# First FFN of a hybrid decoder layer: temporaries in other room, masks in one tile, activation differences on VectorE, output evictions two products later

## The chip, the cores and the metric

The kernel runs on one core of one Trainium2 chip. The metric is the device time of one execution in microseconds (us). The engines are TensorE (PE, with its weight loads as PEld), VectorE (DVE), ScalarE (ACT), GpSimd (POOL) and SyncE (SP, which here only issues DMAs).

## What is computed

One layer on 1024 tokens of width 1024, with 16 learned meta tokens ahead of them, everything in float32:

```python
h = h + 0.5 * swiglu(rms_norm(h, ffn1_norm[l]), ffn1_w_in[l], ffn1_w_out[l])
u = rms_norm(h, mix_norm[l]) @ w_in[l]
hq, hf, hi, hg, sq, sk, sv = jnp.split(u, ...)
o_hg = hgrn2(hq, hf, hi, hg, lb_all[l], hgrn_out_norm[l], valid)
o_sb = stick_breaking(sq, sk, sv, sb_q_norm[l], sb_k_norm[l], valid)
h = h + jnp.concatenate([o_hg, o_sb], axis=-1) @ w_out[l]
h = h + 0.5 * swiglu(rms_norm(h, ffn2_norm[l]), ffn2_w_in[l], ffn2_w_out[l])

def swiglu(h, w_in, w_out):          # D_FF = 2816
    g, u = jnp.split(h @ w_in, 2, axis=-1)
    return (jax.nn.silu(g) * u) @ w_out
```

## The kernel before

**Exactness.** Each float32 operand of a product is split into a rounded high part and a low remainder. ACT casts the high part and DVE subtracts it to get the low one: L360 and L362 for the weights of the first FFN (`wh`, `wl`), L310 and L311 for its activations (`halve`), L612 and L613 in the output pass (`w`, `t`). A product takes three passes, high by high, low by high and high by low. With four blocks of 128 in the contraction, one product of the FFN is 12 matmuls of 128x512.

**Products by halves.** The two FFNs are computed with seven products in the place of eight, on operands divided in halves (a Strassen-Winograd scheme). The activation's halves are B11, B21, B22 and the combinations T1, T2, T3, T4. Weights are combined by POOL (L384, `s`) and activations by DVE. In `fast_in`, a *quad* is the 2x2 blocks of one gate or up column group, and a *pair* is a gate quad and an up quad. The 22 column groups of the first FFN are 11 pairs, named 0 to 10 here. The results of a quad are put together in PSUM banks qa, qb and qc (L430). `u2` (L462) reads the bank qb after the product T2, ahead of the product T3, which adds to the same bank. ACT applies silu, and DVE multiplies gate and up into `sg`.

The products of a pair, `act` B11 to B22, go to DRAM and are read again by the output pass. `combined()` also makes the four combinations T1 to T4 of these. Its subtractions are L533 (T1, T2, T4) and L540 (T3), its DMAs L529. The tile `t` that holds T1, T2 and T4 has two buffers (`t_bufs`, 2), so T4 takes T1's buffer. In the kernel before, both the subtractions and the DMAs are on POOL.

**The opening.** `open_tokens` loads the token rows, scales them by their norm, turns them on PE, and makes T1 to T4 and B11 to B22. Pairs 0 to 3 are the *openers*. Their eight quads take part in the opening: the products B11 and B21 come first, while the second half of the tokens is still prepared, then T2 for each quad, and after `open_ev()` the rest, in turns of a gate and an up quad (`in_turns`). The temporaries `b11, b21, b22, t2, t3` lie in a pool `temps`. At the end of `open_tokens` come the halves of T1, T4 and B22. `open_ev()` then closes `temps` and opens three pools in its room: `ev1` (tiles of the evictions), `turn` and `early` (raw weight blocks of openers' up quads). The causal masks of the later attention are cut by POOL with affine selections on one tile `sd`, one level of seven after the other (L129, L133), each begun by a memset on DVE and ended by a copy on DVE.

**The output pass.** `fast_out` makes seven steps (A12, A11, S1, S2, S4, S3, A22), each with `q` over blocks of the contraction, and adds the result of each to `hT` by four evictions on DVE (L678). A step's evictions come right behind its last product. Weights and activations pass through a ring of 6 tiles.

**Order.** PE's order is the order of the code. In the opening the order of ACT, DVE and SP is the order of the code too (`manual_schedule`), elsewhere the tile scheduler sets it by priority. The projection for the stick-breaking heads (`sb_project`) copies its k, v and q chunks (`use_k`, `use_v`, `use_q`) with ACT and turns v on PE (flip, L1312).

Of the kernel before, what the change touches and what calls it, by code (L numbers as in the profile page):

```python
# [40 lines left out]
class Block:  # L41
# [19 lines left out]
    def setup(self):  # L61
        nc, a = self.nc, self.a
        self.loads = []
        self.const = c = self.pool("const")
        c.tile([P, 80], F32, name="base")
        self.pool("edge", side="right").tile([P, 504], F32, name="edge")
# [28 lines left out]
        self.ss = c.tile([P, 9, 2], F32, name="ss_x")  # L95
        self.sd = c.tile([P, P], F32, name="sd")
        self.ng1 = c.tile([P, KT], F32, name="ng1")
# [14 lines left out]

    def setup_masks(self):
        nc = self.nc
        nc.vector.tensor_copy(self.ident_b, self.ident)
        nc.vector.memset(self.neg_b, 0.0)
        nc.gpsimd.affine_select(
            out=self.neg_b, in_=self.neg_b, pattern=[[-1, P]],
            compare_op=ALU.is_gt, fill=NEG, base=0, channel_multiplier=1,
        )  # L120
        yield
        sd = self.sd
        for i, n in enumerate(LEVELS):
            nc.vector.memset(sd, 1.0)
            nb = P // (2 * n)
            for h in range(2):
                v = sd.rearrange("s (b h r) -> s b h r", h=2, r=n)[:, :, h, :]
                at = n * (1 - h)
                nc.gpsimd.affine_select(  # L129
                    out=v, in_=v, pattern=[[-2 * n, nb], [0, n]],  # L130
                    compare_op=ALU.is_ge, fill=0.0, base=-at, channel_multiplier=1,
                )
                nc.gpsimd.affine_select(  # L133
                    out=v, in_=v, pattern=[[2 * n, nb], [0, n]],
                    compare_op=ALU.is_gt, fill=0.0, base=at + n, channel_multiplier=-1,
                )
            yield
            nc.vector.tensor_copy(self.masks[:, i, :], sd)

# [210 lines left out]
    def fast_in(self, ops, n, w_in, actD, openers, ev0, open_ev, feed=None, meta=None, spare=None,  # L350
                between=lambda: None, after_opened=lambda: None, taken=lambda at, step=True: None):

# [137 lines left out]
        def pair(f, opened=None):  # L490
# [33 lines left out]
            def combined():  # L524

                sub = nc.gpsimd.tensor_sub

# [52 lines left out]
    def fast_out(self, hT, cs, n, w_out, actD, ready, between=lambda a, q: None,  # L580
# [37 lines left out]
        def left(step, q):  # L618
# [26 lines left out]

        banks = {}
        steps = [
# [5 lines left out]
        for bank, a, b, start, (i, j) in steps:  # L653
# [4 lines left out]
            for q in range(nq):  # L658
                src, blocks = left(a, q)
                act = right((q, b), n)  # L660
                with self.tc.high_priority() if self.apart and a == "A12" and q < 3 else ExitStack():
                    wh, wl = halved(src, "w", 512)
                    xh, xl = halved(act, "t", n)
                order = [(m, e) for m in range(4) for e in range(3)]
                if a == "A12" and q == 0:
                    order.sort(key=lambda me: me[1])
                for m, e in order:
                    y, z = ((wh, xh), (wl, xh), (wh, xl))[e]
                    nc.tensor.matmul(  # L669
                        banks[bank][m], y[:, m * P : (m + 1) * P], z,  # L670
                        start=start and q == 0 and e == 0,
                        stop=q == nq - 1 and e == 2, skip_group_check=True,
                    )
                meta(a, q, blocks)
                between(a, q)
            for m in range(4):
                h = hT[:, 4 * i + m, cs[j] : cs[j] + n]
                self.evicted = nc.vector.scalar_tensor_tensor(  # L678
                    h, banks[bank][m], 0.5, h, ALU.mult, ALU.add
                )  # L680
            ready(a)

# [9 lines left out]
    def row_sum(self, row, i, junk, eng):  # L692
        nc, m = self.nc, row.shape[0]
        s = self.ss[:m, i, 0:1]
        if eng is nc.vector:
            eng.scalar_tensor_tensor(
                junk[1][:m], row, 1.0, row, ALU.mult, ALU.mult, accum_out=s
            )
        else:
            nc.scalar.activation(junk[0][:m], row, AF.Square, accum_out=s)  # L700

# [23 lines left out]

    def open_tokens(self, ops, opened, rows_at, pool, operands):

# [22 lines left out]

        def apart(name):
# [14 lines left out]

        ra = rows_in(0)
        for i in range(3):
            self.row_sum(ra[i], i, junk, nc.vector if i == 1 else nc.scalar)
            self.row_root(ra[i], i)  # L770
# [67 lines left out]
        def sums(i):  # L838
            self.row_sum(rb[i], 4 + i, junk, nc.vector)

# [8 lines left out]
        items.update({12 + j: lambda j=j: second(j) for j in range(4)})  # L849
        items.update({8 + j: lambda j=j: combine(j) for j in range(4)})  # L850
        masks = self.setup_masks()
        after = {6: turn_b22, 7: turn_b12, 8: turn_meta}
        for i in range(2, len(order)):
            if i + 2 < len(order):
                next(order[i + 2])
            items[i]()
            if i > 4:
                next(masks, None)
# [350 lines left out]
    def sb_project(self, p, xh, xl, pool, mix, dst):  # L1209
# [27 lines left out]
        yield from self.project(xh, xl, 2048 + P * p, HALVES[: 1 if p == 0 else 2], use_q, w)  # L1237
        yield "start", done[1]
# [341 lines left out]
    def run(self):  # L1580
# [21 lines left out]
        with ExitStack() as c0:  # L1602
            with ExitStack() as c1:
# [8 lines left out]
                with tc.manual_schedule(engines={nc.tensor.engine}), ExitStack() as c2:  # L1612
                    ev0 = self.pool("ev10", ctx=c2)
                    self.ahead = self.pool("ahead", ctx=c2)
                    self.wq = self.pool("w1", ctx=c2)
                    before, rows_at = ExitStack(), ExitStack()
                    temps = self.pool("temps", ctx=before)
                    xa = self.pool("x_ops", ctx=c2, side="right")
# [59 lines left out]
                    def open_ev():  # L1678
                        with ExitStack() as c4:
                            for ins in marks.values():  # L1680
                                c4.enter_context(tc.issue_after(ins))
                            self.setup_rest()
                        before.close()
                        ev = self.pool("ev1", ctx=c2)
                        turning.append(self.turn_x(self.pool("turn", ctx=c2), xD))
                        self.early_raw = self.pool("early", ctx=c2)
                        turning.append(ahead_of_time(self.ahead))
                        return ev

                    marks = {}  # L1690

                    def taken(at, step=True):
# [15 lines left out]
                        ops, n, a["ffn1_w_in"][0], act1D, 4, ev0, open_ev, None, begin, spare,  # L1708
                        lambda: next(turning[0], None), taken=taken,
                    )  # L1710
                    opened = next(steps)
                    with tc.manual_schedule(
                        engines={nc.scalar.engine, nc.vector.engine, nc.sync.engine}
                    ):
                        self.open_tokens(
                            ops, opened, rows_at, temps,
                            lambda: operands(
                                self.pool("t_ops", ctx=c2, side="right"),
                                ("B22", "T4", "T1", "T3", "T2"),
                            ),  # L1720
# [5 lines left out]
                with tc.manual_schedule(engines={nc.tensor.engine}), ExitStack() as c2:  # L1726
# [460 lines left out]
```

## Time and profile before

| | us |
|---|---|
| median of 3 runs | 2056.03 (2050.37 to 2060.83) |
| profiled execution | 2054.86 |
| its span | 2053.2 |
| PE busy | 1980.8 (96%) |
| DVE busy | 1365.5 (67%) |
| ACT busy | 867.2 (42%) |
| POOL busy | 656.9 (32%) |
| mean granted clock of TensorE | 0.991 |

Rough stages of the profiled execution, in us from the start: opening 0 to 116, rest of the openers' pairs to 225, pairs 4 to 10 to 515, output pass of the first FFN to 750, early projections to 781, then both attentions and projections, second FFN in from 1405, its output pass from 1830 to the end.

A row of a timeline reads: start, duration (of all joined instructions), engine, line, operation, out<-in, shapes, count, and in brackets the idle time ahead of it and what released it. A row of waits reads: who waited for whom, the total, the times, the longest. A row of groups reads: count, busy time and mean ns of one, idle time ahead and its releasers.

### The profile page before, as it was taken

How to read it: one execution, taken by the hardware profiler on the slowest of the kernel's cores; microseconds unless marked ns; L12 is line 12 of the kernel's file. 1: busy time of each engine (PE TensorE's matmuls, PEld its weight loads, DVE VectorE, ACT ScalarE, POOL GpSimd, SP SyncE). 2: the span in 40 equal slices, each digit the busy share in tenths (PEclk: the TensorE clock that was granted, in tenths of full speed). 3: DMA queues.
4: the chain of work that ended last, by engine and by line, in shares of the span. 5: the costliest groups of instructions: out<-in, count | busy, mean ns of one | idle time of the engine just before them, and what ended most of it. 6: DMA issues, size and time to landing. Idle time of an engine off the chain costs nothing.

```text
span 2053.2 us, 30869 instructions
## 1 busy us (share of the span) xinstructions
PE 1980.8 (96%) x11004; PEld 1659.7 (81%) x11004; DVE 1365.5 (67%) x2004; ACT 867.2 (42%) x1758; POOL 656.9 (32%) x752
## 2 busy tenths in 40 slices
PE   7699999999999999999999998999999999999998
PEld 6488888877778888898989887877888888888887
DVE  6776677877586763236777658548476676676774
ACT  6332343433244444346666644435133333344443
POOL 1366455544100001224433333320264454440000
PEclk9899999999999999999999999999999999999999
DMA  6145488655895513634444346684632332369463
GB/s 186 60 151 180 158 285 265 242 192 198 302 318 174 159 65 123 190 114 140 142 129 127 93 162 203 171 252 140 204 118 93 108 108 93 107 225 319 130 200 137
DMA packets 283097, 347.18 MB, mean 169 GB/s; under 512 B 28016, under 2 KB 183152, under 8 KB 282944
## 3 DMA queue, kind: packets, MB, share of 16 engines
q1 hardware_dynamic: 263376, 287.98, 44.3%
q0 software_dynamic: 18528, 57.23, 7.9%
q8 instruction: 87, 1.43, 0.3%
q14 instruction: 66, 0.54, 0.1%
q10 hardware_dynamic: 1040, 0.00, 0.0%
HBM read 233.75 MB, written 111.38 MB: 168 GB/s over the span
## 4 chain that ended last, share of the span: by engine, by line
PE 67%; DVE 3%; DMA 2%; ACT 1%; issue 1%; SPq 0%; DVEq 0%; ACTq 0%
PE o L669 18%; PE qb L430 9%; PE qc L430 6%; PE qa L430 6%; PE proj L251 5%; PE proj L253 5%; PE proj L252 5%; PE flip L1312 2%; PE wo L251 1%; PE wo L252 1%; PE wo L253 1%; DMA raw<-in_ffn_w_out_dram 1%; PE lvl L1108 1%; PE oacc L1382 1%; PE oacc L1384 1%; PE z L1448 1%
## 5 line engine op out<-in xcount | busy, mean ns | idle before, releaser
L430 PE MATMUL qb<-T,wh 128*128 128x512 f32 x1056 | 349.6, 395 | 22.8 <-ACT wh L360 14.9
L362 DVE TENSOR_TENSOR wl<-s,wh 128x512 fp32r<-128x512 f32 x160 | 213.0, 1332 | 69.7 <-ACT wh L360 67.4
L430 PEld LDWEIGHTS qb<-T,wh 128*128 128x128 f32 x1056 | 200.8, 190 | 69.9 <-ACT wh L360 15.3
L430 PE MATMUL qa<-B,wh 128*128 128x512 f32 x696 | 228.9, 393 | 1.4 <-ACT both L454 1.4
L669 PE MATMUL o<-t,w 128*128 128x512 f32 x924 | 216.1, 394 | 5.3 <-DVE w L613 2.3
L251 PE MATMUL proj<-xh,wh 128*128 128x512 f32 (+2 forms) x640 | 216.6, 338 | 0.8 <-DVE st L1008 0.7
L253 PE MATMUL proj<-xl,wh 128*128 128x512 f32 (+2 forms) x640 | 209.7, 328 | 0.8 <-DVE xl L1768 0.8
L430 PE MATMUL qb<-T,wl 128*128 128x512 f32 x528 | 208.0, 394 | 2.5 <-DVE wl L362 2.5
L669 PEld LDWEIGHTS o<-t,w 128*128 128x128 f32 x924 | 173.4, 189 | 45.2 <-DVE w L613 4.6
L252 PE MATMUL proj<-xh,wl 128*128 128x512 f32 (+2 forms) x640 | 210.0, 328 | 0.0
L669 PE MATMUL o<-parts 128*128 128x512 f32 x924 | 209.9, 389 | 0.0
L360 ACT CAST wh<-s 128x512 fp32r<-128x512 f32 x160 | 99.4, 622 | 247.0 <-PE qb L430 161.2
L669 PEld LDWEIGHTS o<-parts 128*128 128x128 f32 x924 | 173.4, 188 | 35.9
L384 POOL TENSOR_TENSOR s<-raw 128x512 f32<-128x512 f32 x80 | 112.8, 1412 | 133.1 <-DMA raw<-in_ffn_w_in_dram 53.5
L430 PEld LDWEIGHTS qa<-B,wh 128*128 128x128 f32 x696 | 130.7, 188 | 29.4 <-ACT both L454 2.3
L430 PE MATMUL qa<-B,wl 128*128 128x512 f32 x348 | 135.5, 389 | 0.0
L253 PEld LDWEIGHTS proj<-xl,wh 128*128 128x128 f32 x640 | 120.6, 188 | 12.2 <-DVE xl L1768 1.2
L360 ACT CAST wh<-raw 128x512 fp32r<-128x512 f32 x120 | 74.4, 621 | 132.5 <-PE qc L430 92.4
L251 PEld LDWEIGHTS proj<-xh,wh 128*128 128x128 f32 x640 | 120.8, 189 | 11.4 <-DVE st L1008 1.2
L252 PEld LDWEIGHTS proj<-xh,wl 128*128 128x128 f32 x640 | 120.7, 189 | 9.1
L1464 POOL TENSOR_TENSOR sig<-sig,keep 128x144 f32<-128x144 f32 (+3 forms) x64 | 81.3, 1272 | 134.1 <-DVE keep L1458 85.5
L430 PEld LDWEIGHTS qb<-T,wl 128*128 128x128 f32 x528 | 100.6, 191 | 23.8 <-DVE wl L362 3.4
(387 smaller groups left out, 4120.5 us busy)
## 6 DMA issues: line engine op xcount, KB each, us to landing
raw<-in_ffn_w_in_dram SPq DMA_DIRECT2D x176, 256.0 KB, 3.9
raw<-in_ffn_w_out_dram SPq DMA_DIRECT2D x121, 256.0 KB, 4.6
w2in<-both SPq DMA_DIRECT2D x28, 512.0 KB, 3.1
raw<-in_w_in_dram SPq DMA_DIRECT2D x25, 512.0 KB, 4.1
ks<-kD SPq DMA_DIRECT2D x32, 260.0 KB, 4.9
wout<-both SPq DMA_DIRECT2D x16, 512.0 KB, 4.1
wh<-w2in SPq DMA_DIRECT2D x27, 256.0 KB, 3.4
wl<-w2in SPq DMA_DIRECT2D x27, 256.0 KB, 3.2
```

What stands on the lines that cost most here:

```text
L251: nc.tensor.matmul(ps, wh[:, s], xs, start=k == 0, stop=False)
L252: nc.tensor.matmul(ps, wl[:, s], xs, start=False, stop=False)
L253: nc.tensor.matmul(ps, wh[:, s], xl[:, k, c0 : c0 + n], start=False, stop=k == nk - 1)
L360: nc.scalar.copy(hi, src)
L362: nc.vector.tensor_sub(lo, src, hi.bitcast(F32))
L384: taken(op(t, x, y), False)
L430: nc.tensor.matmul(ps, a[:, k, :], b[:, k, :], start=start and k == 0 and i == 0, stop=k == 3 and i == 2, skip_group_check=True,)
L669: nc.tensor.matmul(banks[bank][m], y[:, m * P : (m + 1) * P], z, start=start and q == 0 and e == 0, stop=q == nq - 1 and e == 2, skip_grou ...
L1108: nc.tensor.matmul(ps[:, :, c, :], kp[:, P * c : P * c + P], strided(QA, P * c + n, (512 - n, 2), (2 * n, nb), (1, n)), start=True, stop=True,
L1312: self.nc.tensor.transpose(ps[:m, j, :], src[:, s0 : s0 + m], self.ident)
L1382: nc.tensor.matmul(o[:, c], vj, w[0], start=j == 0, stop=False, skip_group_check=True)
L1464: nc.gpsimd.tensor_mul(sig, sig, keep[:, 1 : nk + 1])
```

## The change

1. The pools `turn`, `early` and `ev1` are opened ahead of the temporaries and have room of their own. The temporaries go to pools of their own (`b21`; `t2, b11, t3`; `sd`), and `b22` to tiles of `ev1`. They are closed one by one, and the operands T1 to B22 are allocated in three parts. The openers' gate quads, no longer the up quads, use `early`. The subtraction for T2 is done in `combine`, and the halves of T1, T4 and B22 are made in `later()`, one part for each round of `in_turns`.
2. The masks are cut in one tile of seven levels, with one memset on DVE, one block of POOL selections after the last row sum, and one copy on DVE.
3. In the first FFN the subtractions of `combined()` are on DVE. Their DMAs stay on POOL, and `t` keeps two buffers.
4. In both output passes the first three products of A12 are ordered by pass and then by product, and the evictions of a step come behind the second product of the next step, except for S3 and A22. In the first FFN the ring has 7 tiles and `spread` one buffer.
5. In the first `sb_project` the copies have another order, and the first half of the q projection comes ahead of the flips of v.

The changed program's order, by its build: on DVE, T4's subtraction comes behind T1, T2 and T3 and one weight split. In pairs 3 to 6 it comes ahead of the next `u2`, in pairs 7 to 9 behind it, and in pair 10 among the splits of A12. PE's order changes only in points 4 and 5.

```diff
-    def setup_masks(self):
+    def masks_blank(self, sd):
+        nc.vector.memset(sd, 1.0)
...
+    def masks_cut(self, sd):
...
         for i, n in enumerate(LEVELS):
-            nc.vector.memset(sd, 1.0)
...
-            yield
-            nc.vector.tensor_copy(self.masks[:, i, :], sd)
@@ fast_in
-                sub = nc.gpsimd.tensor_sub
+                sub = (nc.vector if meta else nc.gpsimd).tensor_sub
...
-                quad(f * P, gate, opened, 1 * turned, kept[0]),
-                quad(D_FF + f * P, up, opened and "second", 2 * turned, kept[1]),
+                quad(f * P, gate, opened, 2 * turned, kept[0]),
+                quad(D_FF + f * P, up, opened and "second", 1 * turned, kept[1]),
...
                 rounds += 1
+                late()
@@ fast_out
+        delayed, opening = [], []
+        def evict(bank, i, j, step):
...
+                if a == "A12" and q < 3:
+                    opening += order
+                    order = sorted(opening, key=lambda o: (o[1], o[2])) if q == 2 else []
...
-            for m in range(4):
-                h = hT[:, 4 * i + m, cs[j] : cs[j] + n]
-                self.evicted = nc.vector.scalar_tensor_tensor(
-                    h, banks[bank][m], 0.5, h, ALU.mult, ALU.add
-                )
-            ready(a)
+                if q == 1 and delayed:
+                    evict(*delayed.pop())
+            if a in ("S3", "A22"):
+                evict(bank, i, j, a)
+            else:
+                delayed.append((bank, i, j, a))
@@ open_tokens
-        b11, b21, b22, t2, t3 = (apart(x) for x in ("b11", "b21", "b22", "t2", "t3"))
+        b21 = apart("b21", self.pool("b21", ctx=pools["b21"]))
+        temps = self.pool("temps", ctx=pools["t2"])
+        t2, b11, t3 = (apart(x, temps) for x in ("t2", "b11", "t3"))
+        b22 = [ev.tile([P, 512], F32, tag=x, name="b22", bufs=1 + (x == "t"))
+               for x in ("t", "t", "sg01", "sg10")]
+        sd = self.pool("sd", ctx=pools["masks"]).tile([P, len(LEVELS), P], F32, name="sd")
...
             stt(t3[j], ps, self.ng1[:, j : j + 1], b22[j], ALU.mult, ALU.add)
+            sub(t2[j], b22[j], b11[j])
...
-                operands()
-            sub(t2[j], b22[j], b11[j])
+                pools["masks"].close()
+                operands("T1", "T3", "T2")
...
+            if i == 3:
+                with self.tc.issue_after(at.ins):
+                    self.masks_cut(sd)
+        def combined(j):
+            if j == 1:
+                nc.vector.tensor_copy(self.masks, sd)
+            combine(j)
...
-        left = iter((("T1", b11), ("T4", b21), ("B22", b22)))
-        for o, b in left:
+        def later():
             for j in range(4):
-                if o == "T4":
-                    sub(b21[j], b21[j], t2[j])
-                self.halve(ops[o], b[j], j)
+                self.halve(ops["T1"], b11[j], j)
+            yield
+            for j in range(4):
+                sub(b21[j], b21[j], t2[j])
+            pools["t2"].close()
+            operands("T4")
+            for j in range(4):
+                self.halve(ops["T4"], b21[j], j)
+            yield
...
@@ sb_project
-            for ci, (c0, n) in enumerate(CHUNKS):
-                use_v(self.early["v"][ci], ci, c0, n)
-                use_k(self.early["k"][ci], ci, c0, n)
+            for use, x, ci in ((use_k, "k", 0), (use_v, "v", 1), (use_v, "v", 2), (use_v, "v", 0),
+                               (use_k, "k", 1), (use_k, "k", 2)):
+                use(self.early[x][ci], ci, *CHUNKS[ci])
...
+        rest = self.project(xh, xl, 2048 + P * p, HALVES[: 1 if p == 0 else 2], use_q, w)
+        if p == 0:
+            yield next(rest)
         yield "start", done[0]
-        yield from self.project(xh, xl, 2048 + P * p, HALVES[: 1 if p == 0 else 2], use_q, w)
+        yield from rest
@@ the caller
+                    turn = self.pool("turn", ctx=c2)
+                    self.early_raw = self.pool("early", ctx=c2)
+                    ev1 = self.pool("ev1", ctx=c2)
...
-                        before.close()
-                        ev = self.pool("ev1", ctx=c2)
-                        turning.append(self.turn_x(self.pool("turn", ctx=c2), xD))
-                        self.early_raw = self.pool("early", ctx=c2)
+                        turning.append(self.turn_x(turn, xD))
...
-                    self.ring_bufs, self.act_bufs, self.apart = 6, 5, True
+                    self.ring_bufs, self.act_bufs, self.apart = 7, 5, True
...
-                        rs = pn.tile([P, n], F32, tag="spread", name="rs", bufs=2)
+                        rs = pn.tile([P, n], F32, tag="spread", name="rs", bufs=1)
```

More of the change, by code (lines that the diff above doesn't have):

```diff
@@ L64, in setup @@
         self.const = c = self.pool("const")
-        c.tile([P, 80], F32, name="base")
+        c.tile([P, 208], F32, name="base")
         self.pool("edge", side="right").tile([P, 504], F32, name="edge")
@@ L350, in fast_in @@
     def fast_in(self, ops, n, w_in, actD, openers, ev0, open_ev, feed=None, meta=None, spare=None,
-                between=lambda: None, after_opened=lambda: None, taken=lambda at, step=True: None):
+                between=lambda: None, after_opened=lambda: None, late=lambda: None, taken=lambda at, step=True: None):
         nc = self.nc
@@ L646, in fast_out @@
         banks = {}
+        delayed, opening = [], []
+        def evict(bank, i, j, step):
+            for m in range(4):
+                h = hT[:, 4 * i + m, cs[j] : cs[j] + n]
+                nc.vector.scalar_tensor_tensor(
+                    h, banks[bank][m], 0.5, h, ALU.mult, ALU.add
+                )
+            ready(step)
         steps = [
@@ L663, in fast_out @@
                     xh, xl = halved(act, "t", n)
[L664 to L667, printed above, removed]
+                order = [(m, e, q, wh, wl, xh, xl) for m in range(4) for e in range(3)]
+                if a == "A12" and q < 3:
+                    opening += order
+                    order = sorted(opening, key=lambda o: (o[1], o[2])) if q == 2 else []
+                for m, e, at, wh, wl, xh, xl in order:
                     y, z = ((wh, xh), (wl, xh), (wh, xl))[e]
@@ L670, in fast_out @@
                         banks[bank][m], y[:, m * P : (m + 1) * P], z,
-                        start=start and q == 0 and e == 0,
+                        start=start and at == 0 and e == 0,
                         stop=q == nq - 1 and e == 2, skip_group_check=True,
@@ L695, in row_sum @@
         if eng is nc.vector:
-            eng.scalar_tensor_tensor(
+            return eng.scalar_tensor_tensor(
                 junk[1][:m], row, 1.0, row, ALU.mult, ALU.mult, accum_out=s
             )
-        else:
-            nc.scalar.activation(junk[0][:m], row, AF.Square, accum_out=s)
+        return nc.scalar.activation(junk[0][:m], row, AF.Square, accum_out=s)
     def row_root(self, row, i):
@@ L724, in turned, with open_tokens @@
         return ps
-    def open_tokens(self, ops, opened, rows_at, pool, operands):
+    def open_tokens(self, ops, opened, rows_at, ev, operands):
         nc, x = self.nc, self.a["x"][0]
@@ L749, in rows_in, with apart @@
             return got
-        def apart(name):
+        pools = {x: ExitStack() for x in ("b21", "t2", "masks")}
+        def apart(name, pool):
             return [pool.tile([P, 512], F32, name=f"{name}{j}") for j in range(4)]
-        b11, b21, b22, t2, t3 = (apart(x) for x in ("b11", "b21", "b22", "t2", "t3"))
+        b21 = apart("b21", self.pool("b21", ctx=pools["b21"]))
[4 more added lines that the diff above has]
+        sd = self.pool("sd", ctx=pools["masks"]).tile([P, len(LEVELS), P], F32, name="sd")
         kept = {}
@@ L767, in open_tokens @@
         ra = rows_in(0)
+        self.masks_blank(sd)
         for i in range(3):
@@ L849, in open_tokens @@
         items.update({12 + j: lambda j=j: second(j) for j in range(4)})
-        items.update({8 + j: lambda j=j: combine(j) for j in range(4)})
-        masks = self.setup_masks()
+        items.update({8 + j: lambda j=j: combined(j) for j in range(4)})
         after = {6: turn_b22, 7: turn_b12, 8: turn_meta}
@@ L856, in open_tokens @@
             items[i]()
-            if i > 4:
-                next(masks, None)
             next(order[i])
             after.get(i, lambda: None)()
-        left = iter((("T1", b11), ("T4", b21), ("B22", b22)))
-        for o, b in left:
+        def later():
             for j in range(4):
-                if o == "T4":
-                    sub(b21[j], b21[j], t2[j])
-                self.halve(ops[o], b[j], j)
+                self.halve(ops["T1"], b11[j], j)
[7 more added lines that the diff above has]
+            yield
+            pools["b21"].close()
+            operands("B22")
+            for j in range(4):
+                self.halve(ops["B22"], b22[j], j)
+            yield
+        return later()
     def meta_in(self, marks):
@@ L1708, in run @@
                         ops, n, a["ffn1_w_in"][0], act1D, 4, ev0, open_ev, None, begin, spare,
-                        lambda: next(turning[0], None), taken=taken,
+                        lambda: next(turning[0], None), late=lambda: next(later, None),
+                        taken=taken,
                     )
@@ L1714, in run @@
                     ):
[L1715 to L1719, printed above, removed]
+                        later = self.open_tokens(
+                            ops, opened, rows_at, ev1,
+                            lambda *names: operands(
+                                self.pool(names[0] + "_ops", ctx=c2, side="right"), names
                             ),
```

13 lines of the change are left out of this document (5 added, 8 removed).

## The prediction

> **What bounds the kernel now.** I read the page first, then all waits of PE, then the stages in which the change has a hand.
>
> ```profile
> span 2053.2 us, 30869 instructions
> PE 1980.8 (96%) x11004; PEld 1659.7 (81%) x11004; DVE 1365.5 (67%) x2004; ACT 867.2 (42%) x1758; POOL 656.9 (32%) x752
> ```
> TensorE (PE) is busy for 96% of the span, so only what PE waits for, and the clock at which it runs, can move the time. The waits of PE between 60 and 600 us, in the columns total, times, longest:
>
> ```profile
> PE qb L430 <- ACT wh L360: 14.9, 1, 14.9
> PE qb L430 <- DVE u L462: 6.6, 2, 3.8
> PE qb L430 <- DVE wl L362: 2.5, 1, 2.5
> PE o L669 <- DVE w L613: 2.3, 3, 1.2
> PE o L669 <- ACT w L612: 1.6, 1, 1.6
> PE qa L430 <- ACT both L454: 1.4, 2, 0.8
> PE o L669 <- DVE t L613: 1.2, 1, 1.2
> ```
> The 14.9, 2.5 and 1.4 lie in the opening, the 6.6 in the pairs of the first FFN, the rows of L669 in its output pass: 30.5 us in all, and nearly all that the change can win lies in them and in the slow clock behind them.
>
> **The opening.** From the timeline at 70 to 97 us:
>
> ```profile
> 71.54 2.48 DVE L311 TENSOR_TENSOR T<-b,T 128x512 fp32r<-128x512 f32 x4
> ...
> 76.67 2.02 SPq L373 DMA_DIRECT2D raw<-in_ffn_w_in_dram  x4
> ...
> 81.84 5.70 DVE L311 TENSOR_TENSOR B<-b,B 128x512 fp32r<-128x512 f32 x4
> ...
> 81.95 1.71 POOL L384 TENSOR_TENSOR s<-raw 128x512 f32<-128x512 f32 x1 [9.47 <-DMA raw<-in_ffn_w_in_dram]
> ...
> 86.03 0.80 PE L430 MATMUL qb<-T,wh 128*128 128x512 f32 x1 [14.89 <-ACT wh L360]
> ...
> 89.28 0.80 PE L430 MATMUL qb<-T,wl 128*128 128x512 f32 x1 [2.45 <-DVE wl L362]
> ...
> 93.71 1.06 PE L430 MATMUL qb<-T,wh 128*128 128x512 f32 x2
> ...
> 95.46 0.39 PE L430 MATMUL qb<-T,wl 128*128 128x512 f32 x1
> ...
> 96.15 0.39 PE L430 MATMUL qb<-T,wl 128*128 128x512 f32 x1
> ```
> PE stops at 71.14 because the up quad's second weight operand has no raw blocks: SP issues them at 76.67 only, since their tiles reuse the room of the temporaries, POOL combines them from 81.95, PE goes on at 86.03. The product of 12 matmuls that stands there ends with the first of the two at 93.71, thus about 94.14. At full clock three matmuls take 96.15 − 95.46 = 0.69 us, so 12 take 2.76, and the product would have ended at 73.9. Stall, second stall and slow clock together cost 20.2 us.
>
> The change gives `early`, `turn` and `ev1` room of their own, and the openers' gate quads, not the up quads, use `early`. The loads no longer wait for the temporaries, so all 20.2 can go. It also moves the halving of T2's input forward (`sub t2` in `combine`), which may end the two short waits of PE on `both` (L454, 1.4 us above): at most 21.6. What comes in the place of the gap: the halves of T1, T4, B22 move beside products. On DVE these are 8 instructions of T, 4 of B and 4 subtractions at 0.62 to 0.69 (four in 2.48 us), 16 × 0.67 = 10.7 us, until now in PE's gap. I put 27 us of products (ten of 2.76) ahead of the first use of T1's operand. POOL's weight combinations run there too: the B halves took 5.70 for four beside them, against 2.48 for T's four without. So DVE is near full, and I charge 2.4 us. The mask selections on POOL become one block behind the last row sum, with one copy on DVE. So far (busy us, mean ns) they took
>
> ```profile
> L129 POOL TENSOR_SCALAR_AFFINE_SELECT sd<-sd 128x64 f32<-128x64 f32 x14 | 6.9, 513 | 10.3 <-DVE sd L124 10.3
> L133 POOL TENSOR_SCALAR_AFFINE_SELECT sd<-sd 128x64 f32<-128x64 f32 x14 | 5.6, 423 | 0.0
> ```
> 12.5 us in all. The first FFN needs no mask, and the copy stands behind the first `combine`: I take 0, since the block can run under the products ahead of T2's; if DVE waits for most of it, with T2's operands queued behind, up to 9. Gain of the opening: 19.2, from 10 to 21.6.
>
> **Pairs 4 to 10, where the change adds a wait.** `combined()` makes T1, T2, T3, T4 of a pair. The tile `t` has two buffers, so T4's waits until T1's DMA has landed. So far that wait stood on POOL, with little behind it. Now it stands on DVE. In the changed program's order, T4 of pairs 3 to 6 comes ahead of `u2` (L462) of the next gate quad, and PE's product T3 accumulates in the bank that `u2` must have read. Rows at pair 4, then those of pairs 5 and 6 (DMA rows: the last number is us from issue to landing):
>
> ```profile
> 259.82 0.68 DVE L177 TENSOR_TENSOR both<-early,both 128x512 fp32r<-128x512 f32 x1
> ...
> 261.14 5.51 SPq L154 DMA_DIRECT2D early<-in_w_out_dram  x2
> ...
> 261.97 0.56 POOL L529 DMA_DIRECT2D act14T<-t  x1 [0.31 <-POOL t L533]
> ...
> 263.25 0.39 PE L430 MATMUL qb<-T,wh 128*128 128x512 f32 x1
> ...
> act14T<-t POOLq DMA_DIRECT2D x1, 256.0 KB, 6.1
> ...
> 300.87 0.68 DVE L177 TENSOR_TENSOR both<-early,both 128x512 fp32r<-128x512 f32 x1
> ...
> 305.19 0.39 PE L430 MATMUL qb<-T,wh 128*128 128x512 f32 x1
> act15T<-t POOLq DMA_DIRECT2D x1, 256.0 KB, 5.6
> ...
> 342.68 0.68 DVE L177 TENSOR_TENSOR both<-early,both 128x512 fp32r<-128x512 f32 x1
> ...
> 347.00 0.39 PE L430 MATMUL qb<-T,wh 128*128 128x512 f32 x1
> act16T<-t POOLq DMA_DIRECT2D x1, 256.0 KB, 5.6
> ```
> Pair 4: T1 follows L177 on DVE, 260.5 to 261.15; POOL issues its DMA 0.3 later (the row's own idle), 261.4; landing + 6.1 = 267.5; T4 and `u2`, 0.68 each, end at 268.9. PE's T3 was due at 263.25: 5.6 us late. Pair 5: 300.87 + 0.68 + 0.68 + 0.3 + 5.6 + 1.36 = 309.5 against 305.19, 4.3. Pair 6: 351.3 against 347.00, 4.3. Sum 14.2. The transfers are slow there because SP has put weight loads and writes in front (the row of 261.14); the change leaves these in place.
>
> A stall of that size also slows the clock. The granted clock (the third number from the right) in 4 us behind three of today's stalls:
>
> ```profile
> 435.04:439.04 4.00, 4.00 (x12) 3.23 (x13) 4.00 (x4) 0.00 (x0) 2.76 (x3) 0.66 0.42 170
> 481.02:485.02 4.00, 4.00 (x11) 3.20 (x12) 4.00 (x4) 0.00 (x0) 2.73 (x3) 0.61 0.41 168
> 537.46:541.46 4.00, 3.78 (x10) 2.79 (x11) 3.77 (x6) 2.65 (x5) 0.00 (x0) 0.66 0.86 286
> ```
> 4 × (1 − 0.66) = 1.4 to 1.6 us each: three new stalls cost 4.5 more. In pairs 7 to 9 `u2` stands ahead of T4 and does not wait; 0.3 is left for pair 7.
>
> The other way, POOL no longer subtracts beside DVE. Today's two stalls on L462 come from that:
>
> ```profile
> 430.84 3.46 DVE L362 TENSOR_TENSOR wl<-s,wh 128x512 fp32r<-128x512 f32 x1
> ...
> 434.22 0.68 DVE L462 TENSOR_TENSOR u<-qb,p 128x512 f32<-128x512 f32 x1
> ```
> A subtraction of 0.68 took 3.46 beside POOL's, and `u2` came late by it. The Trainium skill ("GPSIMD Engine Reference", section Key points) says that GpSimd shares its SBUF interfaces with VectorE and contends with instructions that have two SBUF inputs; the row agrees. Without POOL's part DVE must itself do T1, T2 and T3 (3 × 0.68) before: I expect 2.0 of the 3.83 us back at pair 8, and at pair 9 its 2.75, of which 0.5 stays, with 1.5 of clock: 5.8 together. If both went with their clock it were 6.6 + 3.0 = 9.6. Pairs 4 to 10: −14.2 − 4.5 − 0.3 + 5.8 = −13.2; bounds: nothing lost at T4's wait, +9.6; as at pair 4 in all seven pairs, −7 × (5.6 + 1.5) = −50. I take the three pairs, since for these the rows give landing, order and due time. Pairs 0 to 3 cost 0.5: T1 lands in 2.3 there and T4 is ready before `u2` is due, but DVE carries 16 more instructions.
>
> **Output pass and projection.** The four evictions of a bank stood on DVE ahead of the next splits:
>
> ```profile
> 590.62 2.47 DVE L678 SCALAR_TENSOR_TENSOR hT<-o,hT 128x512 f32<-128x512 f32 x4
> ```
> Moved two products later, they stop delaying L613; of the 2.3 + 1.2 (L613) and 1.6 (L612) of waits and 1.4 of clock behind 537 I take 4.0, since the splits at the start now compete with the last pair's subtractions; from −1 to 6.5. In the second FFN's output PE had no wait over 0.3 us: 0. The first half of the q projection goes ahead of the flips, whose wait for the third copy of v was 1.3 us: +1.3, from 0.5 to 1.9.
>
> ```profile
> PE flip L1312 <- ACT vTs L1222: 1.3, 1, 1.3
> ```
>
> **Sum.** 19.2 − 0.5 − 13.2 + 4.0 + 1.3 = 10.8 us saved. The profiled execution took 2054.9 us (span 2053.2 and 1.7 around it): 2044. The median of the runs is 2056.0, 1.1 more: **2045 us**. About 0.5%, 10 us, is what a measurement of this kernel can tell from no change, so the forecast stands on that edge.
>
> **Rivals.**
> (1) T4's wait on DVE is short everywhere. T1's DMA of pair 0, with little traffic, landed in 2.3 us, that of pair 8 in 2.9:
>
> ```profile
> act10T<-t POOLq DMA_DIRECT2D x1, 256.0 KB, 2.3
> ...
> act18T<-t POOLq DMA_DIRECT2D x1, 256.0 KB, 2.9
> ```
> If the earlier issue puts T1 ahead of SP's transfers in pairs 4 to 6 too, it lands at 261.4 + 2.3 = 263.7, `u2` ends at 265.1, and the three stalls are 1.9 each, too short to slow the clock by much. With 9.6 from pairs 8 and 9 the total is 19.2 − 0.5 − 5.7 + 9.6 + 4.0 + 1.3 = 27.9: 2028. Against it stand the three rows of 5.6 to 6.1, just where the wait counts. The Trainium skill ("DMA: Bandwidth & Descriptors", the table of cost components) gives about 2.0 us and the bytes at 436 GB/s for a transfer, which for 256 KB I estimate at 2.6. By that rule this rival would hold; the rows of pairs 4 to 6 differ from it.
> (2) Slower: T4's wait becomes the bound in more pairs. It stands on DVE in every pair and the weight splits (L362) are queued behind it. If pairs 7 and 10, where L462 or the output pass's splits follow it, lose 5.6 + 1.5 each as pair 4 does and the gains of 8 and 9 do not come, the pairs cost 14.2 + 4.5 + 14.2 = 32.9, less 24 gained elsewhere: 8.9 slower, 2065. It decides for slower from 24 us on, 3.4 a pair; with all seven pairs alike it is 2082. For it: DVE is the busiest engine after PE, and gets 44 instructions more. Against: only three of the orders put T4 ahead of `u2`.
> (3) The opening's gap only moves: loads come early, but DVE, with the 10.7 us of halves beside splits stretched by POOL, becomes late for T1 or T4, and only 6 of the 19.2 us are kept: 2.4 slower, 2058. For it: 5.70 us for the B halves. Against: the products ahead of them last 27 us.
>
> **How the numbers follow.** Forecast 0.50, its own range 2034 to 2057; (1) 0.20; (2) 0.16; (3) 0.14. The forecast's cases split at 2046: 0.28 faster by over 0.5%, 0.20 within, 0.02 slower. With (1) faster, (2) slower and (3) mostly within: faster 0.49, within 0.32, slower 0.19. The range from 2020 to 2065 holds forecast, (3), most of (1) and half of (2).
>
> **What would show it.** Right: PE's wait on L360 of 14.9 us is gone and T1's halves lie beside products; at pairs 4, 5, 6 PE waits 4 to 6 us for L462, with DVE idle before T4's subtraction until T1's DMA; no DVE subtraction above 2 us near 430 and 477; waits on L669 under 1.5 us in sum. Wrong: no such wait at pairs 4 to 6 (then rival 1), waits of 3 us or more in most pairs (rival 2), or new gaps of over 8 us in sum between 72 and 116 (rival 3).

## The result, and the profile after

The changed kernel takes 2043.3 us in the median of 8 runs (2038.1 to 2047.7), the kernel before 2056.0. The ratio is 0.9939, with a 95% interval of 0.9920 to 0.9957: 0.6% faster, 12.7 us between the medians. The forecast was 2045.

The profiled execution of the changed kernel took 2047.7 us, the longest of its eight, and that of the kernel before was 1.2 us under its median, so the two profiles differ by 7.2 us of span only. The head of the changed kernel's page, and the longest waits of PE over the whole run (who waited for whom, total, times, longest):

```profile
span 2046.0 us, 30906 instructions
...
PE 1982.2 (97%) x11004; PEld 1660.6 (81%) x11004; DVE 1350.3 (66%) x2036; ACT 869.5 (42%) x1758; POOL 595.8 (29%) x708
...
PE qb L428 <- DVE u L460: 18.0, 5, 5.2
PE xps L730 <- POOL sd L129: 11.2, 1, 11.2
...
PE qa L428 <- ACT T L308: 1.8, 1, 1.8
```
Compare these with the rows of before. The 14.9 us on `wh` are gone. The wait on `u` (L462 before, L460 now) went from 6.6 us in two places to 18.0 in five. The 11.2 us on `sd` are the start of the kernel, where PE waited 11.0 us before too. In the output pass of the first FFN no wait of PE is left. POOL lost 61 us of work. DVE, which took 44 instructions over, is busy for 15 us less, since its own instructions are stretched less often: the 160 weight splits that read `s` took 1.33 us on average before and take 1.12.

PE runs 11,004 matmuls in both kernels, in the same order but for points 4 and 5, so the start of its k-th matmul marks the same place in both. From the two traces, in us:

| stretch | matmuls of PE | before | after | difference |
|---|---|---|---|---|
| start | to 0 | 11.0 | 11.2 | +0.2 |
| opening | 0 to 300 | 86.3 | 66.5 | −19.7 |
| rest of the openers | 300 to 1290 | 158.7 | 159.7 | +1.0 |
| pairs 4 to 6 | 1290 to 2050 | 131.9 | 154.8 | +22.9 |
| pairs 7 to 10 | 2050 to 2650 | 113.7 | 110.1 | −3.6 |
| output pass of the first FFN | 2650 to 4150 | 269.1 | 261.0 | −8.2 |
| q projection | 4150 to 4350 | 34.0 | 32.3 | −1.6 |
| all that follows | 4350 to the end | 1248.4 | 1250.3 | +1.9 |

**Pair 4 after.** From the timeline, with the rows of PE at pairs 5 and 6 at the end:

```profile
242.16 0.68 DVE L531 TENSOR_TENSOR t<-sg 128x512 f32<-128x512 f32 x1
...
243.14 0.54 POOL L527 DMA_DIRECT2D act14T<-t  x1 [2.02 <-DVE t L531]
...
243.64 7.53 SPq L152 DMA_DIRECT2D early<-in_w_out_dram  x2
...
248.28 0.69 DVE L531 TENSOR_TENSOR t<-sg,t 128x512 f32<-128x512 f32 x1 [3.51 <-DMA act14T<-t]
248.88 0.68 DVE L460 TENSOR_TENSOR u<-qb,p 128x512 f32<-128x512 f32 x1
...
249.71 0.77 PE L428 MATMUL qb<-T,wh 128*128 128x512 f32 x1 [4.90 <-DVE u L460]
...
299.64 0.77 PE L428 MATMUL qb<-T,wh 128*128 128x512 f32 x1 [5.23 <-DVE u L460]
...
348.44 0.76 PE L428 MATMUL qb<-T,wh 128*128 128x512 f32 x1 [4.99 <-DVE u L460]
```
T1 is made at 242.16 and its DMA issued at 243.14. DVE stands for 3.51 us until that DMA has landed, makes T4, then `u2`, and only then PE goes on, after a stall of 4.90 us. At pairs 5 and 6 the same stall is 5.23 and 4.99. The DMA rows of T1 in pairs 4, 5 and 6 (last number: us from issue to landing):

```profile
act14T<-t POOLq DMA_DIRECT2D x1, 256.0 KB, 5.0
...
act15T<-t POOLq DMA_DIRECT2D x1, 256.0 KB, 6.3
...
act16T<-t POOLq DMA_DIRECT2D x1, 256.0 KB, 6.4
```
And the granted clock (third number from the right) in the 4 us behind each stall:

```profile
249.71:253.71 4.00, 4.00 (x10) 3.13 (x11) 1.66 (x3) 0.00 (x0) 0.10 (x1) 0.50 0.68 242
299.64:303.64 4.00, 4.00 (x10) 3.18 (x11) 1.66 (x3) 0.00 (x0) 0.10 (x1) 0.55 0.48 197
348.44:352.44 4.00, 4.00 (x10) 3.13 (x11) 1.65 (x3) 0.00 (x0) 0.10 (x1) 0.50 0.48 197
```
The slow clock does not end with these 4 us at pairs 4 and 6. From the end of each stall to the end of its slow clock:

```profile
249.71:255.48 5.77, 5.77 (x18) 4.55 (x22) 1.93 (x4) 0.22 (x1) 0.10 (x1) 0.50 0.58 210
299.64:303.26 3.62, 3.62 (x9) 2.85 (x10) 1.66 (x3) 0.00 (x0) 0.10 (x1) 0.50 0.53 217
348.44:354.46 6.02, 6.02 (x22) 4.78 (x26) 2.18 (x4) 0.48 (x1) 0.10 (x1) 0.50 0.32 131
```
These are 15.4 us at half clock, which cost 7.7 us. With the stalls of 15.1 us they make the 22.9 us of that stretch.

**The opening after.** The halves that filled PE's gap now lie beside products. From the groups of DVE between 66 and 116 us (busy us, mean ns):

```profile
L309 DVE TENSOR_TENSOR T<-b,T 128x512 fp32r<-128x512 f32 x7 | 5.0, 750 | 0.0
...
L309 DVE TENSOR_TENSOR B<-b,B 128x512 fp32r<-128x512 f32 x4 | 2.6, 678 | 0.0
...
L890 DVE TENSOR_TENSOR b<-b,t 128x512 f32<-128x512 f32 x3 | 2.0, 678 | 0.0
```
The B halves took 5.70 us for four before and take 2.6 now.

### The profile page after: what moved, and what is told of

It is laid out like the page before. It is cut to its first block, busy times and chain, and to the rows that moved or that the text cites. A ratio compares the mean times of both kernels' runs of the same rounds, so it can differ in the third digit from the quotient of the medians.

```text
span 2046.0 us, 30906 instructions
## 1 busy us (share of the span) xinstructions
PE 1982.2 (97%) x11004; PEld 1660.6 (81%) x11004; DVE 1350.3 (66%) x2036; ACT 869.5 (42%) x1758; POOL 595.8 (29%) x708
## 4 chain that ended last, share of the span: by engine, by line
PE 82%; DVE 6%; DMA 4%; issue 3%; ACT 2%; POOL 2%; SPq 0%; DVEq 0%; POOLq 0%; ACTq 0%
PE o L679 19%; PE qb L428 16%; PE qc L428 11%; PE qa L428 9%; PE proj L249 5%; PE proj L251 5%; PE proj L250 5%; PE flip L1351 2%; PE wo L249 1%; PE wo L250 1%; PE wo L251 1%; PE mq L935 1%; DMA raw<-in_ffn_w_out_dram 1%; PE lvl L1144 1%; PE oacc L1421 1%
## 5 line engine op out<-in xcount | busy, mean ns | idle before, releaser
L360 DVE TENSOR_TENSOR wl<-s,wh 128x512 fp32r<-128x512 f32 x160 | 179.3, 1121 | 56.5 <-ACT wh L358 54.4
```

The lines of the kernel that those rows point to most:

```text
L360: nc.vector.tensor_sub(lo, src, hi.bitcast(F32))
```

## The experiments

The theory was that the change gains in the opening, the output pass and the projection, and gives most of it back in pairs 4 to 6, because T4's wait for T1's DMA stands on DVE ahead of `u2`. The rivals were the load that 44 more subtractions put on DVE, the other parts of the change that move transfers, and the place of T4's wait against the wait itself. The stretches from the traces, in us, columns as in the rows of the table above:

| kernel | opening | pairs 4 to 6 | pairs 7 to 10 | output pass | q projection |
|---|---|---|---|---|---|
| before | 86.3 | 131.9 | 113.7 | 269.1 | 34.0 |
| after | 66.5 | 154.8 | 110.1 | 261.0 | 32.3 |
| T4 in place | 66.4 | 133.9 | 110.4 | 260.9 | 32.3 |
| subtractions on POOL | 65.9 | 132.9 | 117.0 | 262.2 | 32.3 |
| before, subtractions on DVE | 84.7 | 150.9 | 109.9 | 269.9 | 34.0 |
| point 4 undone | 66.7 | 154.7 | 107.2 | 265.2 | 32.3 |
| T4 alone on POOL | 67.1 | 132.5 | 109.2 | 262.3 | 32.3 |
| steps held back | 66.5 | 131.8 | 109.7 | 295.9 | 32.3 |
| DMAs issued by ACT | 66.4 | 147.7 | 115.2 | 262.1 | 32.3 |
| quads swapped back | 68.1 | 152.4 | 108.5 | 261.6 | 32.3 |
| point 5 undone | 66.3 | 154.5 | 107.4 | 262.0 | 34.0 |
| T4 on POOL, masks copied early | 65.9 | 132.4 | 107.4 | 261.8 | 32.3 |

**1. T4 in place, without the wait.**

```diff
-                put("T4", made(sg[1, 0], t2))
+                if meta:
+                    sub(sg[1, 0], sg[1, 0], t2)
+                    put("T4", sg[1, 0])
+                else:
+                    put("T4", made(sg[1, 0], t2))
```

> The changed kernel, but T4 is written in place over sg10 and no longer takes T1's buffer: the same subtractions on DVE, no wait for T1's DMA. If that wait is the cost: PE's three stalls of 4.9 to 5.2 us at pairs 4 to 6 and their slow clock go, the pairs 4 to 10 no longer lose 19.3 us against the kernel before but gain up to 9, and the time falls by 20 to 28 us from the changed kernel's 2043, to 2015 to 2023. If the load of DVE by the 44 subtractions is the cost: stalls of 3 us or more stay there and the time stays within 6 us of 2043.

2024.0 us, ratio to the kernel before 0.9853 (0.9838 to 0.9867). The waits of PE between 225 and 520 us:

```profile
PE qb L428 <- DVE u L460: 5.4, 4, 1.9
PE qb L428 <- DVE wl L360: 1.1, 2, 0.6
```
Of 18.0 us on `u` 5.4 are left, none over 1.9. Pairs 4 to 6 fall from 154.8 to 133.9 us with the same subtractions on DVE, and T1's DMA lands there after 5.9 to 6.3 us, as late as in the changed kernel. So the wait costs these 21 us, not DVE's load, to which 2.0 us against the kernel before are left at most. The total lies just above the range that I had given for this case.

**2. The subtractions on POOL again.**

```diff
-                sub = (nc.vector if meta else nc.gpsimd).tensor_sub
+                sub = nc.gpsimd.tensor_sub
```

> The changed kernel, but the subtractions of combined() are on POOL again. If the subtractions on DVE cost what the pairs lose: pairs 4 to 10 take as long as in the kernel before, with its two stalls of 3.8 and 2.8 us at pairs 8 and 9, and the time is 19 us under the changed kernel, about 2024. If the longer pairs come from elsewhere in the change (the transfers that start earlier): the stalls at pairs 4 to 6 stay and the time is within 5 us of 2043.

2028.5 us, 0.9876 (0.9857 to 0.9894). The stalls at pairs 4 to 6 are gone, the two at pairs 8 and 9 (3.86 and 3.03 us) are back:

```profile
PE qb L428 <- DVE u L460: 6.9, 2, 3.9
```
The stalls at pairs 4 to 6 come with the subtractions on DVE. The time is 4 us above what I expected. Pairs 7 to 10 took 117.0 us, longer than in either kernel: the granted clock over the 4 us behind the two stalls was 0.50, against 0.66 and 0.61 in the kernel before.

**3. The kernel before with the subtractions on DVE.**

```diff
-                sub = nc.gpsimd.tensor_sub
+                sub = (nc.vector if meta else nc.gpsimd).tensor_sub
```

> The kernel before with point 3 alone: the subtractions of combined() of the first FFN on DVE. If T4's wait on DVE is the cost and depends on nothing else of the change: stalls of 4 to 6 us at pairs 4 to 6 and 17 to 20 us more than before, 2073 to 2076. If the wait is only long because the rest of the change has moved the transfers: less than 6 us more than before.

2070.7 us, 1.0081 (1.0066 to 1.0096): 15.8 us more than the kernel before beside it. Its waits at pairs 4 to 6 were 4.78, 4.10 and 3.91 us:

```profile
PE qb L430 <- DVE u L462: 14.7, 4, 4.8
```
The cost is a little under what I expected, with 19.0 us in pairs 4 to 6. Point 3 alone makes the kernel slower; it needs no other part of the change for that.

**4. Point 4 undone.**

```diff
-                if a == "A12" and q < 3:
...
+                if a == "A12" and q == 0:
+                    order.sort(key=lambda me: me[1])
...
-                if q == 1 and delayed:
-                    evict(*delayed.pop())
...
-                    self.ring_bufs, self.act_bufs, self.apart = 7, 5, True
+                    self.ring_bufs, self.act_bufs, self.apart = 6, 5, True
```

> The changed kernel with point 4 undone in both output passes (A12 product by product, evictions at the end of each step, ring of 6). The profile gave the output pass of the first FFN a gain of 8.2 us, of which I had forecast 4.0. If the point gives it: the stretch is 8 us longer again, with waits on the splits of 1.2 us at its start, 1.6 at 536 and 0.9 and 1.2 at the evictions, 2051. If a part of the 8.2 comes from the subtractions on DVE that no longer slow the splits at the pass's start: 4 to 6 us longer, 2047 to 2049.

2043.9 us, 0.9948 (0.9931 to 0.9965): under both forecasts, and by the time alone not to be told from the changed kernel. In the trace the output pass is 4.3 us longer than after (265.2 against 261.0), with these waits:

```profile
PE o L668 <- DVE w L612: 2.6, 4, 1.9
PE o L668 <- ACT w L611: 0.6, 2, 0.4
```
The eight kernels that have point 4 and its usual transfers take 260.9 to 262.3 us there, so in this pass the point is worth about 3 to 4 us, and some 4 of the pass's 8.2 come with the rest of the change. They are not from the subtractions on DVE alone: the kernel of experiment 3 has these, and its pass takes 269.9; and with them on POOL again, in experiment 2, it takes 262.2. In experiment 3 the six splits of A12 stand on DVE behind the last `u` of pair 10, as in the kernel before, and here ahead of it. Why the scheduler sets them otherwise was not tried.

**5. T4 alone on POOL.**

```diff
-                def made(x, y):
+                def made(x, y, sub=sub):
...
-                put("T4", made(sg[1, 0], t2))
+                put("T4", made(sg[1, 0], t2, nc.gpsimd.tensor_sub))
```

> The changed kernel, but T4's subtraction alone is on POOL again: T1, T2, T3 on DVE, the two buffers of t and with them the wait for T1's DMA as they are. If only the place of the wait costs (DVE, with u2 behind it): no stall of over 1.5 us at pairs 4 to 6 and 2022 to 2028, near the kernel without the wait (2024). If the wait costs by the late T4 itself, wherever it is made: stalls at pairs 4 to 6 stay and the time is 2035 or more.

2021.2 us, 0.9832 (0.9813 to 0.9852). At pair 4:

```profile
243.59 0.68 DVE L460 TENSOR_TENSOR u<-qb,p 128x512 f32<-128x512 f32 x1
...
244.42 0.47 PE L428 MATMUL qb<-T,wh 128*128 128x512 f32 x1
...
248.28 1.72 POOL L531 TENSOR_TENSOR t<-sg,t 128x512 f32<-128x512 f32 x1 [3.06 <-DMA act14T<-t]
```
T4 still waits 3.06 us for T1's DMA, which lands after 6.2, but POOL has nothing behind it that PE waits for. `u2` runs on DVE at 243.59, well before T1's DMA has landed, and PE's product T3 follows at 244.42. No stall over 0.6 us is left at pairs 4 to 6. The wait costs by its place, not by the late T4.

**6. The transfers held back.**

```diff
-                    first, hooks, steps_ahead = 32, 54, 54
+                    first, hooks, steps_ahead = 57, 30, 54
```

> The changed kernel, but the ahead-of-time steps (loads and writes of later weights by SP) are held back in pairs 4 to 6 and made in pairs 7 to 10 at nearly twice the rate. If these transfers make T1 land late: in pairs 4 to 6 T1's DMA takes 2.3 to 3.5 us in the place of 5.0 to 6.4, and PE's stalls there fall under 2 us; pairs 7 to 10 get transfers of 5 us or more and may stall instead, so the total says little. If T1 lands late for another reason (its own queue on POOL, the other DMAs of the pair): still 5 us or more there and stalls of 4 us.

T1's DMA in pairs 4, 5 and 6:

```profile
act14T<-t POOLq DMA_DIRECT2D x1, 256.0 KB, 2.9
...
act15T<-t POOLq DMA_DIRECT2D x1, 256.0 KB, 2.4
...
act16T<-t POOLq DMA_DIRECT2D x1, 256.0 KB, 2.7
```
With the same instructions for T1 to T4 on DVE, pairs 4 to 6 take 131.8 us and have no stall. (The steps' own work on DVE is gone there too, 86 instructions in the place of 113 over the same 612 matmuls, but the landing is measured by itself.) At pair 7, where the steps begin, T1 took 5.0 and a stall of 3.6 us appears. So the transfers of SP's steps make T1 late. The total of this one run, 2055.7, shows only that the steps were crowded: PE waits 25 us for them in the output pass.

**7. The DMAs of T1 to T4 issued by ACT.**

```diff
-                    nc.gpsimd.dma_start(actD[f // 2, name], t)
+                    (nc.scalar if meta else nc.gpsimd).dma_start(actD[f // 2, name], t)
```

> The changed kernel, but the DMAs of T1 to T4 are issued by ACT, on a hardware queue, in the place of POOL. If the queue is what is slow in pairs 4 to 6: T1 lands in 2 to 3 us there and the stalls fall under 2 us. If the DMA engines are full with SP's transfers: 4.5 to 6.5 us from issue to landing as with POOL, and stalls of 4 us or more; ACT's issues, which wait for DVE, may add short waits of their own.

```profile
act14T<-t ACTq DMA_DIRECT2D x1, 256.0 KB, 5.0
...
act15T<-t ACTq DMA_DIRECT2D x1, 256.0 KB, 5.8
...
act16T<-t ACTq DMA_DIRECT2D x1, 256.0 KB, 4.9
```
Another queue lands T1 about as late, so POOL's queue is not the cause. PE's stalls there are now waits for ACT, which stands for its own DMA issues with a copy for PE behind them. They are 4.0, 3.3 and 3.2 us:

```profile
PE qa L428 <- ACT p L452: 10.4, 3, 4.0
```
One run, 2042.3 us.

**8. The openers' quads swapped back.**

```diff
-                quad(f * P, gate, opened, 2 * turned, kept[0]),
-                quad(D_FF + f * P, up, opened and "second", 1 * turned, kept[1]),
+                quad(f * P, gate, opened, 1 * turned, kept[0]),
+                quad(D_FF + f * P, up, opened and "second", 2 * turned, kept[1]),
```

> The changed kernel, but the openers' up quads use the tiles of early again and the gate quads the ring, as in the kernel before; early keeps its own room. If the room is what ended the opening's gap of 14.9 us: the 300th matmul of PE starts within 2 us of the changed kernel's 77.7. If the swap of the quads does it: a gap of 5 us or more near 72 us comes back.

The 300th matmul starts at 79.1 us, against 77.7 after and 97.3 before. A wait of 3.5 us stands at 66, and the one of 1.8 at 58 is gone:

```profile
PE qb L428 <- DVE wl L360: 3.5, 1, 3.5
```
So the swap does not end the gap; it is worth 1.4 us more. POOL combines the weights that the gap waited for at 60 us here, at 82 in the kernel before: their loads no longer wait for the temporaries. The room alone was not undone. One run, 2042.3 us.

**9. Point 5 undone.**

```diff
-            for use, x, ci in ((use_k, "k", 0), (use_v, "v", 1), (use_v, "v", 2), (use_v, "v", 0),
...
+            for ci, (c0, n) in enumerate(CHUNKS):
+                use_v(self.early["v"][ci], ci, c0, n)
+                use_k(self.early["k"][ci], ci, c0, n)
...
-            yield next(rest)
```

> The changed kernel with point 5 undone: the copies' old order and the q projection behind the flips. If the point gives the 1.6 us that the profile shows in that stretch: the wait of the flips for v's copy (1.3 us) is back, and the stretch from the 4150th to the 4350th matmul of PE takes 33.9 us as in the kernel before, in the place of 32.3. If the stretch is shorter for another reason: 32.3 to 32.8.

The stretch takes 34.0 us and the flips wait again:

```profile
PE flip L1348 <- ACT vTs L1258: 1.3, 1, 1.3
```
Point 5 gives 1.7 us of this stretch. One run, 2042.9 us.

**10. T4 on POOL, and the masks copied earlier.**

```diff
-                put("T4", made(sg[1, 0], t2))
+                put("T4", made(sg[1, 0], t2, nc.gpsimd.tensor_sub))
...
         def keep_b22():
+            nc.vector.tensor_copy(self.masks, sd)
...
         def combined(j):
-            if j == 1:
-                nc.vector.tensor_copy(self.masks, sd)
```

> T4's subtraction on POOL as in the run before, and the one copy of the masks on DVE earlier, beside keep_b22 at about 40 us, where DVE waits for PE, in the place of the second combine. If the copy of 1.7 us is what made PE's wait of 1.8 to 2.1 us near 59 us: that wait falls under 0.7 us and the time is 1 to 2 us under the 2021 of T4 on POOL alone. If the wait comes from the subtractions of T2 that were moved forward: it stays as it is, and the time too.

2021.4 us, 0.9834 (0.9814 to 0.9855), the same as without the move. PE's wait near 58 us stays, 2.1 us. The copy is not its cause, and the cause is not shown. What stands there on ACT ahead of PE's next `both` are the casts of T2's and T3's halves, which wait for `b` and `t` on DVE; that they hold `both` up is argued from the timeline, and no run tried it.

The kernels of 1, 5 and 10 are the fastest, with 2021 to 2024 us, and their intervals overlap. That of 2, with 2028.5, beats the changed kernel too: each of the four undoes or moves the wait that point 3 put on DVE.

## Why the prediction was right, and where not

Forecast against the profile, by the steps of the sum (us, gain positive):

| step | forecast | profile |
|---|---|---|
| opening | 19.2 | 19.7 |
| openers 0 to 3 | −0.5 | −1.0 |
| pairs 4 to 10 | −13.2 | −19.3 |
| output pass | 4.0 | 8.2 |
| q projection | 1.3 | 1.6 |
| all else | 0 | −2.1 |
| sum of the unrounded terms | 10.8 | 7.2 |

That the medians came within 2 us of the forecast, 2043.3 against 2045, is in part luck: pairs 4 to 10 lost 6.1 us more than forecast, the output pass won 4.2 more, and the two profiled executions lie 5.5 us closer together than the medians.

**The opening** held. One of its terms was wrong: the 1.4 us on `both` were not won. One wait of 1.8 us at 58 took their place. The 2.4 us charged to a full DVE were not lost there, since POOL no longer ran beside the B halves (2.6 us, not 5.70). The two errors cancel. The masks were sized at nothing for a wrong reason too: their selections ran from 2 to 13 us and not behind the last row sum, which DVE made at 31 us.

**The openers** lost 1.0 us, 0.5 forecast. One premise of the 0.5 did not hold: in pairs 0 to 2 T1 landed in 3.3 to 4.7 us, not 2.3, and T4 waited 1.2 to 2.6 us for it. That the 1.0 come from this is not shown, since the kernel of experiment 4, where T4 waits 1.2 to 1.6 us there, takes 158.7 as the kernel before.

**T4's wait** was right in its mechanism, its place and its size: 5.6, 4.3 and 4.3 us forecast, 4.90, 5.23 and 4.99 measured. Experiments 1, 5 and 6 take the stalls away in three ways (another room, another engine, an early landing), and pairs 4 to 6 get 21 to 23 us shorter each time.

**The clock** behind these stalls was mis-sized. I took 1.5 us for each from stalls of 1.6 to 3.8 us and a window of 4 us; behind 5 us the clock was 0.50 for 3.6 to 6.0 us, and the stretch lost (22.9 − 15.1) / 3 = 2.6 us for each. That is 3.3 of the 6.1 us by which pairs 4 to 10 were missed. The stalls themselves, 15.1 us against 14.2, are 0.9 more. The other 1.9 are in pairs 7 to 10, where 3.6 us were won and 5.5 forecast. Single executions differ there: with the same code in this stretch, the kernels of experiments 4, 8 and 9 won 6.5, 5.2 and 6.3. Pair 8 keeps a stall of 1.9 us, as forecast. Behind it the clock over 4 us was 0.62 in the changed kernel's execution, and 1.00 in those three behind stalls of 1.5 to 1.9 us.

**The output pass** gave 8.2 us. Point 4 is 3 to 4 of them by experiment 4, near the 4.0 forecast. That the other points would move the splits at the pass's start was not foreseen.

**The rivals.** Rival 1, a short wait, was wrong for this kernel, and right about its condition: where SP's transfers are held back T1 lands in 2.4 to 2.9 us. The Trainium skill ("DMA: Bandwidth & Descriptors", the table of cost components) gives about that, an estimate of 2.6 from its figures. With SP's transfers T1 takes 5.0 to 6.4, and the measurement decides. Its price was not borne out: it kept three stalls of 1.9 us, and experiment 6 has none there. It also left out the clock behind such stalls, against the forecast's own row of 0.66 behind a stall of 1.60 us at 537.46. Kernels without the stalls run in 2021 to 2024, under the 2028 that I had worked out. Rival 2 needed 24 us lost in pairs 4 to 10, and 19.3 were. At pair 7, T1 took 5.6 us and T4 waited 3.5 for it, but behind `u2`, and PE lost 0.7; the order, not the landing, is what spared it. Rival 3, a DVE too full for the opening, did not come.

The profile's 7.2 us and the medians' 12.7 differ by the two executions that were profiled: the changed kernel's is 4.3 us over its median, that of the kernel before 1.2 under. Some 3 us of this lie in pairs 7 to 10, against experiments 4 and 9. From the 7350th to the 7900th matmul the changed kernel's execution took 93.2 us, against 89.5 to 90.9 in the ten experiments, but that of the kernel before took 92.2, so only 1.0 of the difference lies there. Its cause was not looked for.

## What to carry to other kernels

Moving an operation to a faster engine moves its waits too: look at what it waits for and at what is queued behind it there, before its own duration. Here a subtraction of 0.7 us with a buffer held by a DMA cost 20 us on the engine that PE waits for, and nothing on the idle one or with another buffer. When several edits come together, take each apart by stretches of the same instructions in the traces: 33 us gained in some stretches and 26 lost in others looked like a change of 0.6%.

## What the runs showed of the hardware

- A 256 KB write to DRAM that lands in 2.3 to 2.9 us with little other traffic took 4.9 to 6.4 us behind the loads and writes that SP had issued just before, whether POOL's or ACT's queue carried it (the profiles before and after, experiments 6 and 7). The landing time to plan with is that of the place, not of the transfer.
- The granted clock fell to 0.50 for 3.6 to 6.0 us behind stalls of 4.9 to 5.2 us. Behind stalls of 1.6 to 3.8 us in the kernel before it was 0.61 to 0.66 over 4 us. Behind the stall of 1.9 us at pair 8 it was 0.62 after and 1.00 with T4 in place, so whether a short stall costs the clock differs between executions.
